# One decoder layer on one core: projections, gates and latents written ahead of the delta rule

## The chip, the cores and the metric

The kernel runs on one core of a Trainium2 chip. A core has a matrix engine (TensorE, PE in the rows), a vector engine (VectorE, DVE), a scalar engine (ScalarE, ACT), a general engine (GpSimd, POOL) and a queue engine (SyncE, SP) that here only issues DMAs. Each engine works through its own list of instructions in order and waits on semaphores for the others. The metric is device microseconds of one launch; lower is better.

## What is computed

One layer for 512 tokens of width 1024 in fp32. Cut to what the change touches:

```
proj = rmsnorm(x) @ w_in            # dq dk dv (4 heads of 128), dz, db, da, cq, ckv, kix, wix
q, k, v = silu(causal_conv4(dq, dk, dv));  q, k = l2norm(q) * 128**-0.5, l2norm(k)
# gated delta rule: a triangular solve (I + strict(beta k k^T decay)), then a scan with a state
o_dn = rmsnorm(delta_rule(q, k, v, beta, g)) * silu(dz)
# sparse attention: 8 heads, each query attends to the 128 keys that an indexer scores highest
score = sum_h wix_h * relu(q_idx_h . k_idx), causal;  idx = top_k(score, 128)
o_dsa = softmax(q_abs . c_kv[idx] / 8 + bias) @ c_kv[idx] @ w_uv
x = x + concat(o_dn, o_dsa) @ w_out
# then cross-attention into 256 memory tokens, a SwiGLU block, a last rmsnorm
```

## The kernel before

Most matmuls are in fp32r with every operand split into a high and a low part, three matmuls for one product (`mm3`, L149 to L151; for the gates L506 to L508). A weight block is loaded raw, ACT copies its high part (L141), and POOL or DVE subtracts to get the low part (`wl`, L142). Up to the output projection POOL does this for q, k and v of heads 2 and 3, all v, and the gates' weights.

The stages up to the output projection, by function:

- The indexer: L407/L408 multiply, L414 and L418/L419 (ACT and DVE) apply relu and weight, POOL adds into `masks` (L416), and L421 sets the future to a large negative number. `masks` holds the scores of three tiles of queries, 256, 384 and 512 keys wide.
- `project(kind, h)`: one head's k, q or v: 24 matmuls into one PSUM bank, L367 scales the bank out on DVE, then the four-tap convolution on ACT, DVE (L375, L378, L379) and POOL (L374, L380), and SiLU (L381). q, k of heads 0 and 1 come earlier than the change.
- `topk()`: a generator of 16 steps and a last one. A step takes the eight largest of each of three tiles (MAX8, L489) and strikes them out (L490, a load of the values and a MATCH_REPLACE8). The last step turns `masks` into an additive mask (L493). All of it is on DVE.
- `latents()`: q, k and v of the attention from the low-rank parts (`qd`, `kT`, `vt`; L533, L538 are plain fp32).
- `gates()`: SiLU of dz for four token tiles: 96 matmuls into four PSUM banks at once (L506 to L508), ACT (L512), POOL (L514).
- `prepare(h)`: norms of k and q, K K^T and K Q^T (L662), their products with the decay (L665), and a write of the result to DRAM (`n_d`).
- `diagonal_blocks()`: reads the 16x16 blocks of all heads back, inverts them with a serial chain of small DVE instructions (L691 to L710), writes them out (`x_d`, `y_d`, L712) and gathers them into the diagonals of `X` (SP's queue) and `Y` (ACT's queue, L717).
- `level(0)`, `level(1)`: the inverse grows from 16 to 32 to 64: L726 on PE, L728 on DVE, L734 on PE, L735 on DVE for four heads; level 0 ends with transposes of `Y` (L637) copied to `X` on ACT (L737). `last_level()`: 64 to 128, L745 to L758.
- `values_of(h)`: v with the tokens on the partitions (transposes L637, ACT L676).
- `recurrence()` and `attention()`, generators that run interleaved: four chunks of the scan (L781 to L825; the first chunk begins with L781 on `vtok`, `Y`), and logits (L582/L583), masks and maxima (L592), exponentials (L594), transposes (L598), sums (L607).

In the program text before, `prepare` of heads 0 and 1 comes first, then k and q of heads 2 and 3, each pair with its `prepare`, then the diagonal blocks and the levels, then latents, v, `values_of`, the gates, and the selection (`topk`) at the end. The text isn't the order on the engines: the program is built with a scheduler that simulates the engines and gives every instruction its place in its engine's list by when it is ready in that simulation. So the selection's DVE steps, last in the text, stand between the others from the moment when the scores are there.

What else couples the stages: the PSUM tiles are three `g` (the delta rule), two `lg` and two `tp` (projections, gates, latents; later the attention), one `o`. Weight blocks have three raw buffers and two for each split part. The attention's own buffers reuse those.

Of the kernel before, what the change touches and what calls it, by code (L numbers as in the profile page):

```python
# [81 lines left out]
def hybrid_block(ctx, tc, I, out):  # L82
# [85 lines left out]
    def weights(src, k0, kt, c0, cols, sub=None):  # L168
        return weights_split(*weights_raw(src, k0, kt, c0, cols), sub)
# [18 lines left out]
    xn = pool_of("xn")  # L188
# [113 lines left out]
    for w_, name in ((wq, "w_qidx"), (wu, "w_uq")):  # L302
        raw, _ = weights_raw(I[name][0], 0, 2, 0, 512)
# [46 lines left out]
    cvp = pool_of("cvp")  # L350

    def project(kind, h, bank="mm", sub=pool):
        def c(shape=(128, T)):
            n_t[0] += 1
            return cvp.tile(list(shape), FT, name=f"cp{n_t[0]}", tag="cp", bufs=6)

        m = {"q": h, "k": 4 + h, "v": 8 + h}[kind]
        wh, wl = weights(w_in, 0, 8, m * 128, 128, sub)
        o = dense(wh, wl, XH, XL, o=ps(bank))
        if kind == "k" and QK[h] is None:  # L360
            QK[h] = gdn.tile([128, 2, T], FT, name=f"QK{h}", tag=f"QK{h}")
        if kind == "v":
            vtok[h] = gdn.tile([128, NT, 128], FT, name=f"vtok{h}", tag=f"vtok{h}")
        dst = vtok[h].rearrange("p c d -> p (c d)") if kind == "v" else QK[h][:, 0 if kind == "k" else 1, :]
        cp = c((128, T + 4))
        pool.memset(cp[:, 0:3], 0.0)  # L366
        dve.tensor_tensor(cp[:, 3:T + 3], o, Rrow, op=OP.mult)  # L367
        a, b = c(), c()
        act.activation(a, cp[:, 0:T], AF.Identity, scale=par("conv_w", m))
        if m in (9, 11):  # L370
            d_ = c()
            act.activation(b, cp[:, 1:T + 1], AF.Identity, scale=par("conv_w", 12 + m))
            act.activation(d_, cp[:, 2:T + 2], AF.Identity, scale=par("conv_w", 24 + m))
            pool.tensor_tensor(b, b, d_, op=OP.add)  # L374
            dve.scalar_tensor_tensor(a, cp[:, 3:T + 3], par("conv_w", 36 + m), a, op0=OP.mult, op1=OP.add)  # L375
        else:
            act.activation(b, cp[:, 1:T + 1], AF.Identity, scale=par("conv_w", 12 + m))
            dve.scalar_tensor_tensor(a, cp[:, 2:T + 2], par("conv_w", 24 + m), a, op0=OP.mult, op1=OP.add)  # L378
            dve.scalar_tensor_tensor(b, cp[:, 3:T + 3], par("conv_w", 36 + m), b, op0=OP.mult, op1=OP.add)  # L379
        pool.tensor_tensor(a, a, b, op=OP.add)  # L380
        act.activation(dst, a, AF.Silu)  # L381
# [6 lines left out]
    for pr_ in range(4):  # L388
        q = ps()
# [51 lines left out]
    q = ps()  # L441
# [13 lines left out]
    for h in range(4):  # L455
        q = ps()
# [15 lines left out]
    q = ps()  # L472
# [12 lines left out]
    def topk():  # L485
        m8 = dsa.tile([128, 64], FT, name="m8")[:, :8]
        for it in range(16):
            for t in (3, 2, 1):
                dve.max(m8, score[t])  # L489
                dve.match_replace(score[t], m8, score[t], MARK)  # L490
            yield
        for t in (1, 2, 3):
            dve.tensor_scalar(score[t], score[t], MARK, -NEG, op0=OP.not_equal, op1=OP.mult)  # L493
        yield
# [25 lines left out]
    def latents():  # L520

        u = [gdn.tile([128, 512], FT, name=n, tag=f"zg{i}") for i, n in enumerate(("w_ukT", "w_uvT"))]
        sp.dma_start(u[0], I["w_ukT"])
        sp.dma_start(u[1], I["w_uvT"])
        for pr_ in range(4):
            ms = slice(pr_ * 128, (pr_ + 1) * 128)
            q = ps("mm")
            for k in range(2):
                mm3(q, wu[:, 0, k, ms], wu[:, 1, k, ms], cqh[k], cql[k], k == 0, k == 1)
            qd.append(dsa.tile([128, T], FT, name=f"qd{pr_}", tag=f"od{pr_}"))  # L530
            act.activation(qd[pr_], q, AF.Copy, scale=-0.125)
            q = ps("mm")
            pe.matmul(q, u[0][:, ms], ckvT, start=True, stop=True)  # L533
            kT.append(dsa.tile([128, T], FT, name=f"kT{pr_}", tag=f"ol{pr_}"))
            act.activation(kT[pr_], q, AF.Copy)
        for t in range(NT):
            q = ps("mm")
            pe.matmul(q, ckvT[:, t * 128:(t + 1) * 128], u[1], start=True, stop=True)  # L538
            vt.append(dsa.tile([128, 512], FT, name=f"vt{t}"))
            act.activation(vt[t], q, AF.Copy)  # L540
# [105 lines left out]
    def prepare(h):  # L646
        hc = slice(4 * h, 4 * h + 4)
        rk, cc = small(4), small(4)
        irk[h] = small(4)
        squares(tokens(QK[h][:, 0, :]), rk)  # L650
        rsqrt(rk, rk, 1.0)
        pool.tensor_tensor(cc, rk, rk, op=OP.mult)
        pool.tensor_tensor(cc, cc, beta[:, hc], op=OP.mult)
        pool.tensor_tensor(kdc[:, hc], cc, kd[:, hc], op=OP.mult)
        dve.reciprocal(irk[h], rk)
        for c in range(NT):
            act.activation(Dm[:, h, c, :], Dm[:, h, c, :], AF.Identity, scale=cc[:, c:c + 1])
        for c2 in range(2):
            q = ps("g")
            for e in range(2):  # L660
                c = 2 * c2 + e
                pe.matmul(q[:, 256 * e:256 * e + 256], QK[h][:, 0, c * 128:(c + 1) * 128],  # L662
                          QK[h][:, :, c * 128:(c + 1) * 128], start=True, stop=True)
            for k, dst in enumerate((NTt, A)):
                dve.tensor_tensor(dst[:, h, 2 * c2:2 * c2 + 2, :],  # L665
                                  q.rearrange("p (e k i) -> p e k i", e=2, k=2)[:, :, k, :],
                                  Dm[:, h, 2 * c2:2 * c2 + 2, :], op=OP.mult)
        sp.dma_start(bass.AP(tensor=n_d.tensor, offset=n_d.offset + h * 66048,
                             ap=[[128, 128], [16512, 4], [1, 128]]), NTt[:, h])
        squares(tokens(QK[h][:, 1, :]), ssq_[:, hc])  # L670
        pool.tensor_tensor(QK[h][:, 1, :], QK[h][:, 1, :], row[:, h, :], op=OP.mult)
# [157 lines left out]
    def steps(g, n):  # L829
        for _ in range(n):  # L830
            next(g, None)

    gt = topk()
    NTt = gp.tile([128, 4, NT, 128], FT, name="NTt", tag="NT")
    A = gp.tile([128, 4, NT, 128], FT, name="A", tag="A")
    prepare(0)
    prepare(1)
    for h in (2, 3):
        project("k", h)
        project("q", h)  # L840
        prepare(h)
    X = gp.tile([128, 4, NT, 128], FT, name="X", tag="X")
    Y = gp.tile([128, 4, NT, 128], FT, name="Y", tag="Y")
# [3 lines left out]
    for lev in range(2):  # L847
        level(lev)
    last_level()
    latents()  # L850
    for h in range(4):
        project("v", h)
    for h in range(4):
        values_of(h)
    for g_ in (gates(), gt):
        for _ in g_:
            pass
    cvp.release()
    xn.release()
    OGh = gp.tile([128, 4, T], FR, name="OGh", tag="NT")  # L860
    OGl = gp.tile([128, 4, T], FR, name="OGl", tag="OGl")
    core = recurrence()
# [52 lines left out]
    for k in range(KD):  # L915
        q = ps()
# [117 lines left out]
    g_ = I["g_final"]  # L1034
# [30 lines left out]
    for hf in range(2):  # L1065
        for t in range(NT):
            q = ps()
# [67 lines left out]
```

## Time and profile before

| | |
|---|---|
| device time, median of 3 runs | 860.77 us (859.05 to 861.39) |
| profiled execution | 862.52 us, of which span 860.7 us |
| mean granted clock of PE | 0.981 |
| busy in the span: PE, DVE, ACT, POOL | 828.9, 490.9, 366.5, 209.3 us |

The span is the time from the first to the last instruction in the profile; all times of the rows below count from its start. Busy shares say little by themselves: PE is busy 96% of the span, but DVE, with 57%, is busy without a break in one stretch and half idle in the rest. From about 282 us on (output projection, cross-attention, SwiGLU) PE is busy nearly all the time.

### The profile page before, as it was taken

How to read it: one execution, taken by the hardware profiler on the slowest of the kernel's cores; microseconds unless marked ns; L12 is line 12 of the kernel's file. 1: busy time of each engine (PE TensorE's matmuls, PEld its weight loads, DVE VectorE, ACT ScalarE, POOL GpSimd, SP SyncE). 2: the span in 40 equal slices, each digit the busy share in tenths (PEclk: the TensorE clock that was granted, in tenths of full speed). 3: DMA queues.
4: the chain of work that ended last, by engine and by line, in shares of the span. 5: the costliest groups of instructions: out<-in, count | busy, mean ns of one | idle time of the engine just before them, and what ended most of it. 6: DMA issues, size and time to landing. Idle time of an engine off the chain costs nothing.

```text
span 860.7 us, 11019 instructions
## 1 busy us (share of the span) xinstructions
PE 828.9 (96%) x4122; PEld 685.4 (80%) x4122; DVE 490.9 (57%) x817; ACT 366.5 (43%) x721; POOL 209.3 (24%) x217
## 2 busy tenths in 40 slices
PE   8998989899988999999999999999999999999996
PEld 7876757688776889898887888888888888888885
DVE  7787899974666555364555545553345553345542
ACT  6573774334577444353434443331122332233332
POOL 5448758426231132000002321110011110001122
PEclk9998999998899999999999999999999999999998
DMA  8541322116443534353323523333333333323302
GB/s 286 138 110 50 111 73 48 59 12 153 111 105 89 205 98 126 96 144 100 99 73 99 171 80 91 99 98 98 97 98 99 98 98 98 98 81 91 98 25 97
DMA packets 134940, 88.30 MB, mean 103 GB/s; under 512 B 10304, under 2 KB 122344, under 8 KB 134888
## 3 DMA queue, kind: packets, MB, share of 16 engines
q1 hardware_dynamic: 131848, 85.87, 34.4%
q10 hardware_dynamic: 3040, 1.75, 0.6%
q8 instruction: 32, 0.52, 0.2%
q14 instruction: 20, 0.16, 0.1%
HBM read 76.84 MB, written 4.99 MB: 95 GB/s over the span
## 4 chain that ended last, share of the span: by engine, by line
PE 78%; DVE 10%; ACT 4%; DMA 3%; issue 2%; POOL 2%; SPq 1%; ACTq 0%; POOLq 0%; DVEq 0%
PE ps L149 21%; PE ps L150 21%; PE ps L151 21%; DVE masks L490 1%; DVE m L489 1%; PE ps L607 1%; POOL masks L416 1%; PE ps L1080 1%; PE ps L1079 1%; PE ps L1078 1%; PE ps L954 1%; PE ps L956 1%; PE ps L955 1%; DVE cp L379 1%; PE ps L726 1%
## 5 line engine op out<-in xcount | busy, mean ns | idle before, releaser
L141 ACT ACTIVATE wh<-wraw 128x1024 fp32r<-128x1024 f32 x120 | 127.1, 1061 | 311.5 <-PE ps L150 172.6
L149 PE MATMUL ps<-XH,wh 128*128 128x512 f32 x512 | 200.8, 392 | 0.8 <-ACT wh L141 0.5
L151 PE MATMUL ps<-XH,wl 128*128 128x512 f32 x512 | 200.9, 392 | 0.4 <-POOL cp L366 0.4
L150 PE MATMUL ps<-XL,wh 128*128 128x512 f32 x512 | 200.1, 391 | 0.0
L142 DVE TENSOR_TENSOR wl<-wraw,wh 128x1024 fp32r<-128x1024 f32 x108 | 154.6, 1433 | 66.8 <-ACT wh L141 66.5
L149 PEld LDWEIGHTS ps<-XH,wh 128*128 128x128 f32 x512 | 96.2, 188 | 21.2 <-ACT wh L141 0.9
L151 PEld LDWEIGHTS ps<-XH,wl 128*128 128x128 f32 x512 | 96.2, 188 | 20.3 <-POOL cp L366 0.8
L150 PEld LDWEIGHTS ps<-XL,wh 128*128 128x128 f32 x512 | 96.2, 188 | 19.5 <-issue 0.2
L1049 POOL TENSOR_TENSOR t2k<-t2k,t2k 128x512 f32<-128x512 f32 x22 | 29.4, 1335 | 291.0 <-DVE t2k L1048 283.9
L258 POOL TENSOR_TENSOR acc<-acc,t2k 128x512 f32<-128x512 f32 x21 | 35.8, 1705 | 173.4 <-ACT t2k L257 173.1
L1048 DVE TENSOR_TENSOR t2k<-ps,row 128x512 f32<-128x512 f32 x22 | 15.2, 691 | 67.9 <-PE ps L151 67.9
L151 PE MATMUL ps<-HH,wl 128*128 128x512 f32 x128 | 50.0, 393 | 0.0
L149 PE MATMUL ps<-HH,wh 128*128 128x512 f32 x128 | 49.9, 390 | 0.0
L150 PE MATMUL ps<-HL,wh 128*128 128x512 f32 x128 | 49.6, 390 | 0.0
L1060 DVE TENSOR_TENSOR XR<-ps,XR 128x512 f32<-128x512 f32 x16 | 11.1, 692 | 51.9 <-PE ps L151 51.9
L1046 DVE TENSOR_TENSOR t2k<-ps,row 128x512 f32<-128x512 f32 x22 | 15.2, 691 | 36.0 <-PE ps L151 36.0
L142 POOL TENSOR_TENSOR wl<-wraw,wh 128x1024 fp32r<-128x1024 f32 x12 | 29.4, 2453 | 13.8 <-ACT wh L141 13.8
L489 DVE MAX8 m<-masks 128x8 f32<-128x512 f32 (+2 forms) x48 | 26.7, 556 | 4.3 <-POOL masks L421 3.4
L890 DVE TENSOR_TENSOR XR<-ps,XR 128x512 f32<-128x512 f32 x16 | 10.9, 689 | 31.2 <-PE ps L151 31.2
L150 PEld LDWEIGHTS ps<-HL,wh 128*128 128x128 f32 x128 | 24.0, 188 | 5.0
L151 PEld LDWEIGHTS ps<-HH,wl 128*128 128x128 f32 x128 | 24.0, 188 | 5.0
L149 PEld LDWEIGHTS ps<-HH,wh 128*128 128x128 f32 x128 | 24.1, 188 | 4.9
(398 smaller groups left out, 1673.0 us busy)
## 6 DMA issues: line engine op xcount, KB each, us to landing
wraw<-in_w_gate SPq DMA_DIRECT2D x22, 512.0 KB, 3.6
wraw<-in_w_up SPq DMA_DIRECT2D x22, 512.0 KB, 3.7
wraw<-in_w_down SPq DMA_DIRECT2D x20, 512.0 KB, 3.7
wraw<-in_w_in SPq DMA_DIRECT2D x16, 512.0 KB, 3.7
wraw<-in_w_xkv SPq DMA_DIRECT2D x16, 512.0 KB, 3.7
wraw<-in_w_out SPq DMA_DIRECT2D x8, 512.0 KB, 3.7
wraw<-in_w_xq SPq DMA_DIRECT2D x8, 512.0 KB, 3.8
wraw<-in_w_xo SPq DMA_DIRECT2D x8, 512.0 KB, 3.9
```

What stands on the lines that cost most here:

```text
L141: act.activation(h, src, AF.Copy)
L142: (sub or dve).tensor_tensor(l, src, f32(h), op=OP.subtract)
L149: pe.matmul(o, lh, rh, start=start, stop=False)
L150: pe.matmul(o, lh, rl, start=False, stop=False)
L151: pe.matmul(o, ll, rh, start=False, stop=stop)
L258: pool.tensor_tensor(self.acc, self.acc, s_, op=OP.add)
L489: dve.max(m8, score[t])
L890: dve.tensor_tensor(XR[m], o, XR[m], op=OP.add)
L1046: dve.tensor_tensor(s1, og_, Rrow2, op=OP.mult)
L1048: dve.tensor_tensor(s2, ou_, Rrow2, op=OP.mult)
L1049: pool.tensor_tensor(s1, s1, s2, op=OP.mult)
L1060: dve.tensor_tensor(XR[m], o, XR[m], op=OP.add)
```

## The change

The calls up to the recurrence are put in another order. No operation is added or removed, and no tile changes its size.

```
-    NTt, A = ...                      +    gt = topk()
-    prepare(0); prepare(1)            +    latents()
-    for h in (2, 3):                  +    for i, (kind, h) in enumerate(k2, q2, k3, q3, v0 .. v3):
-        project k, q of h             +        steps(gt, 1 if i % 2 else 2)
-        prepare(h)                    +        project(kind, h)
                                       +    gates() to its end, then topk to its end
                                       +    cvp.release(); xn.release()
                                       +    NTt, A = ...
                                       +    prepare(0) .. prepare(3)
     X, Y, memsets                          X, Y, memsets
     diagonal_blocks(), levels              diagonal_blocks(), levels
-    latents(); project v0 .. v3
     values_of(0 .. 3)                      values_of(0 .. 3)
-    gates() to its end, topk to its end
-    cvp.release(); xn.release()
     recurrence and attention               recurrence and attention
```

The lines themselves:

```
     gt = topk()
+    latents()
+    for i, (kind, h) in enumerate([(k, h) for h in (2, 3) for k in "kq"] + [("v", h) for h in range(4)]):
+        steps(gt, 1 if i % 2 else 2)
+        project(kind, h)
+    for g_ in (gates(), gt):
+        for _ in g_:
+            pass
+    cvp.release()
+    xn.release()
     NTt = gp.tile([128, 4, NT, 128], FT, name="NTt", tag="NT")
     A = gp.tile([128, 4, NT, 128], FT, name="A", tag="A")
-    prepare(0)
-    prepare(1)
-    for h in (2, 3):
-        project("k", h)
-        project("q", h)
+    for h in range(4):
         prepare(h)
```

What the scheduler makes of it is seen in each engine's list. On PE, where level 0 begins, before (`ps_1808` to `ps_1811` are the gates' four banks, `ps_1320` to `ps_1366` belong to level 0):

```order
L637 MATMUL ps_1799<-cst,vtok_1758 128x128 x4
L506 MATMUL ps_1808<-wh_1874,XH_88 128x512
L506 MATMUL ps_1809<-wh_1874,XH_88 128x512
L506 MATMUL ps_1810<-wh_1874,XH_88 128x512
L506 MATMUL ps_1811<-wh_1874,XH_88 128x512
L726 MATMUL ps_1341<-X,NTt 128x128 x4
L734 MATMUL ps_1348<-Y,cv_1325 128x128 x4
L734 MATMUL ps_1354<-Y,cv_1332 128x128 x4
L507 MATMUL ps_1808<-wl_1875,XH_88 128x512
L508 MATMUL ps_1808<-wh_1874,XL_96 128x512
L506 MATMUL ps_1808<-wh_1874,XH_89 128x512
```

The same place after the change (`ps_1412` is the gates' last bank, `ps_1806` to `ps_1858` belong to level 0):

```order
L507 MATMUL ps_1412<-wl_1506,XH_91 128x512
L508 MATMUL ps_1412<-wh_1505,XL_99 128x512
L726 MATMUL ps_1806<-X,NTt 128x128 x4
L726 MATMUL ps_1813<-X,NTt 128x128 x4
L726 MATMUL ps_1820<-X,NTt 128x128 x4
L726 MATMUL ps_1827<-X,NTt 128x128 x4
L734 MATMUL ps_1834<-Y,cv_1811 128x128 x4
L734 MATMUL ps_1840<-Y,cv_1818 128x128 x4
L734 MATMUL ps_1846<-Y,cv_1825 128x128 x4
L734 MATMUL ps_1852<-Y,cv_1832 128x128 x4
L637 MATMUL ps_1858<-cst,Y 128x128 x4
```

Before, the gates' matmuls stand between and behind those of level 0; now all 96 stand ahead of it, and level 0 follows with nothing between its own steps. Level 1 comes directly behind it, with the attention's first logits between its matmuls, and 49 rows of PE lie between the first logits (L582) and the first chunk of the recurrence (L781), where there were 20 before.

On DVE, where the diagonal blocks end (L710), before:

```order
L710 COPY cv_1300<-cv_1276 128x256
L490 MATCH_REPLACE masks<-m_1944,masks 128x256
L489 MAX m_1944<-masks 128x8
L375 SCALAR_TENSOR_TENSOR cp_1762<-cp_1759,prT,cp_1762 128x512
L490 MATCH_REPLACE masks<-m_1944,masks 128x512
L489 MAX m_1944<-masks 128x8
```

and after, up to level 0's first instruction (L728):

```order
L710 COPY cv_1786<-cv_1762 128x256
L490 MATCH_REPLACE masks<-m_991,masks 128x512
L489 MAX m_991<-masks 128x8
L493 TENSOR_SCALAR masks<-masks 128x512
L490 MATCH_REPLACE masks<-m_991,masks 128x384
L489 MAX m_991<-masks 128x8
L493 TENSOR_SCALAR masks<-masks 128x384
L490 MATCH_REPLACE masks<-m_991,masks 128x256
L493 TENSOR_SCALAR masks<-masks 128x256
L728 TENSOR_TENSOR cv_1811<-ps_1806,cst 128x512
```

Before, 36 more rows follow L710 up to the selection's last (L493), with level 0's L728 and L735 among them. Now the selection ends eight rows behind L710, and the levels come after it.

On POOL, where the indexer's scores are added up, before (`wl_1143` is the low part of a later head's weights):

```order
L416 TENSOR_TENSOR masks<-masks,rlb 128x256
L416 TENSOR_TENSOR masks<-masks,rlb 128x384
L416 TENSOR_TENSOR masks<-masks,rlb 128x256
L416 TENSOR_TENSOR masks<-masks,rlb 128x512
L142 TENSOR_TENSOR wl_1143<-wraw_1140,wh_1142 128x1024
L416 TENSOR_TENSOR masks<-masks,rlb 128x256
L416 TENSOR_TENSOR masks<-masks,rlb 128x384
L416 TENSOR_TENSOR masks<-masks,rlb 128x512
L416 TENSOR_TENSOR masks<-masks,rlb 128x384
```

and after:

```order
L416 TENSOR_TENSOR masks<-masks,rlb 128x256
L416 TENSOR_TENSOR masks<-masks,rlb 128x512
L416 TENSOR_TENSOR masks<-masks,rlb 128x384
L416 TENSOR_TENSOR masks<-masks,rlb 128x256
L416 TENSOR_TENSOR masks<-masks,rlb 128x512
L416 TENSOR_TENSOR masks<-masks,rlb 128x384
L416 TENSOR_TENSOR masks<-masks,rlb 128x512
L416 TENSOR_TENSOR masks<-masks,rlb 128x256
L416 TENSOR_TENSOR masks<-masks,rlb 128x384
L421 AFFINE_SELECT masks<-masks 128x128 x2
```

The split of weights has left its place among the additions into `masks`; the next one comes behind the last L421. On PE, a projection's 24 matmuls that stood among the indexer's matmuls have given their place to six plain fp32 matmuls of the latents, and stand behind the indexer now. From the fifth block of the output projection on, PE's lists are the same.

## Rows read from the trace of the kernel before

**Rows 1.** Windows: busy time of each engine, PE clock, DMA, by stage.

```profile
90.00:175.50 85.50, 76.76 (x322) 58.16 (x320) 82.15 (x188) 48.08 (x139) 52.83 (x57) 0.96 0.28 76
175.50:217.50 42.00, 41.00 (x296) 36.72 (x297) 25.97 (x60) 16.82 (x38) 19.33 (x22) 0.88 0.33 80
```

**Rows 2.** Windows of 5 us, the same columns.

```profile
80.00:85.00 5.00, 4.51 (x24) 4.41 (x23) 2.92 (x9) 4.32 (x12) 3.78 (x5) 0.54 0.11 32
...
210.00:215.00 5.00, 5.00 (x36) 4.15 (x33) 2.56 (x8) 3.24 (x11) 0.72 (x1) 0.50 0.82 197
...
235.00:240.00 5.00, 3.67 (x29) 3.26 (x28) 4.11 (x12) 3.83 (x19) 1.41 (x2) 1.00 0.59 141
```

**Rows 3.** Timeline of PE: start, length, instruction, count, idle before and releaser.

```profile
78.89 0.79 PE L407 MATMUL ps<-kid,qst3l 128*128 128x512 f32 x1 [2.51 <-DVE rlb L414]
...
159.62 0.74 PE L506 MATMUL ps<-wh,XH 128*128 128x512 f32 x1 [3.09 <-DVE cp L367]
...
175.59 2.92 PE L726 MATMUL ps<-X,NTt 128*128 128x128 f32 x24 [1.32 <-DMA Y<-y_d]
...
196.87 2.84 PE L726 MATMUL ps<-X,NTt 128*128 128x128 f32 x24
...
204.22 0.41 PE L745 MATMUL ps<-cst,Y 64*64 64x64 f32 x4
...
217.51 1.06 PE L781 MATMUL ps<-vtok,Y 128*128 128x128 f32 x4
...
282.47 0.50 PE L149 MATMUL ps<-odh,wh 128*128 128x512 f32 x1
```

**Rows 4.** Timeline of PE, 89 to 104 us: prices of single kinds of instruction.

```profile
89.46 0.40 PE L150 MATMUL ps<-XL,wh 128*128 128x512 f32 x1
...
94.24 0.39 PE L150 MATMUL ps<-XL,wh 128*128 128x512 f32 x1
...
101.93 0.60 PE L637 MATMUL ps<-cst,QK 128*128 128x128 f32 x4
102.37 1.89 PE L662 MATMUL ps<-QK 128*128 128x256 f32 x8
```

**Rows 5.** Timeline of POOL, in the indexer's stage.

```profile
75.02 2.35 POOL L142 TENSOR_TENSOR wl<-wraw,wh 128x1024 fp32r<-128x1024 f32 x1
```

**Rows 6.** Timeline of DVE, first and last of the selection, and level 1.

```profile
89.51 0.69 DVE L489 MAX8 m<-masks 128x8 f32<-128x512 f32 x1 [3.42 <-POOL masks L421]
...
166.64 2.51 DVE L710 COPY cv<-cv 128x256 f32<-128x256 f32 x1
...
185.68 0.56 DVE L489 MAX8 m<-masks 128x8 f32<-128x384 f32 x1
...
188.72 0.29 DVE L493 TENSOR_SCALAR masks<-masks 128x256 f32<-128x256 f32 x1
...
197.96 0.69 DVE L728 TENSOR_TENSOR cv<-ps,cst 128x512 f32<-128x512 f32 x1 [8.35 <-PE ps L726]
```

**Rows 7.** Groups of DVE by form, 89.4 to 189.6 us: busy, mean ns, idle before.

```profile
L379 DVE SCALAR_TENSOR_TENSOR cp<-cp,prT,cp 128x512 f32<-128x512 f32 x6 | 6.6, 1093 | 0.0
L378 DVE SCALAR_TENSOR_TENSOR cp<-cp,prT,cp 128x512 f32<-128x512 f32 x6 | 5.7, 943 | 0.0
...
L698 DVE TENSOR_TENSOR cv<-cv,cv 128x12 f32<-128x12 f32 x2 | 3.3, 1668 | 0.0
...
L728 DVE TENSOR_TENSOR cv<-ps,cst 128x512 f32<-128x512 f32 x4 | 2.7, 680 | 0.0
L735 DVE TENSOR_TENSOR Y<-Y,ps 128x512 f32<-128x512 f32 x4 | 2.7, 680 | 0.0
...
L375 DVE SCALAR_TENSOR_TENSOR cp<-cp,prT,cp 128x512 f32<-128x512 f32 x2 | 1.5, 740 | 0.0
...
L698 DVE TENSOR_TENSOR cv<-cv,cv 128x16 f32<-128x16 f32 x1 | 0.2, 160 | 0.0
```

**Rows 8.** Timeline of ACT: issue of the gathers into Y.

```profile
170.89 3.90 ACTq L717 DMA_DIRECT2D Y<-y_d  x8
```

More of the change, by code (lines that the diff above doesn't have):

```diff
@@ L849, in hybrid_block @@
     last_level()
-    latents()
-    for h in range(4):
-        project("v", h)
     for h in range(4):
         values_of(h)
[L855 to L859, printed above, removed]
     OGh = gp.tile([128, 4, T], FR, name="OGh", tag="NT")
```

## Prediction

> **What bounds the kernel now.** I read the stage windows first. From 90 to 175.5 us DVE is busy 82.15 of 85.5 us and PE 76.76; from 175.5 to 217.5 us PE is busy 41 of 42 us and DVE 25.97 [rows 1]. So up to the first level DVE sets the pace, and in the levels PE does. DVE's timeline shows why: the selection begins at 89.51 us, after DVE had idled 3.42 us for POOL's additions into the scores, and runs, mixed with convolutions, `prepare` and the diagonal blocks, to its last L493 at 188.72 us [rows 6]. The diagonal blocks' last instruction (L710) ends at 169.15 us in this mix, the gathers into `Y` are issued from 170.89 us [rows 8], and level 0 starts at 175.59 us, released by that DMA [rows 3]: 6.44 us from L710's end to level 0. Then the roles turn: DVE idles 8.35 us before level 1 [rows 6], since on PE the gates' matmuls stand between levels 0 and 1.
>
> PE's timeline gives the waits that the text order leaves: 2.51 us at the end of the indexer, 3.09 us before the gates (their fourth bank waits for a v projection's L367), 1.32 us before level 0 [rows 3]. After a wait the granted clock shows its lower level: 0.54 in 80 to 85 us. But 3.67 busy us out of five in 235 to 240 us, in short gaps, left it at 1.00, and it was at 0.50 in 210 to 215 us, in the last level, with PE busy throughout [rows 2].
>
> From 282.47 us the output projection runs [rows 3], with its order unchanged. So the question is when PE gets there.
>
> **The change, part by part.**
>
> *Start of the selection.* On POOL a split of 2.35 us stood among the additions [rows 5], while PE and DVE waited on that chain (the 2.51 and 3.42 us above). It now stands behind the last L421. The wait of 3.42 us covers the 2.35, so the selection starts 2.4 us earlier, at 87.1 us. At the least nothing, if the convolution or the `Dm` work on POOL takes its place; at the most 3.4 us, the whole idle time.
>
> *DVE's chain up to level 0.* The instructions are the same, but eight of level 0's (L728, L735: 680 ns each [rows 7], about 0.6 us from start to start, so 4.8 us) leave the selection's stretch. It lasted from 89.51 to 189.0 us, 99.5 us; now 94.7, so it ends at 181.8 us. The cost is in the place of L710: before, 36 rows followed it to the selection's end, now eight. By the end of the stretch before (185.68 to 189.0 us with one L735 in it [rows 6], plus a MATCH_REPLACE ahead of it) those eight take about 3.4 us, L493s included. L710 ends near 178.3 us, 9 us later than before, and with the same 6.4 us of DMA level 0 starts at **184.7 us**, 9 us later.
>
> This hangs on the DVE instructions that are stretched while POOL works. The convolution's L379 takes 1093 ns in the mean and L378 943, the same form in L375 740; two tiny L698 took 1668 ns, a third 160 [rows 7]; L710 took 2.51 us. That is 6×0.35 + 6×0.20 + 2×1.51 = 6.3 us of stretch, and with L710 some 8. I keep it, since POOL's list has the same splits near the same DVE rows. If it goes away level 0 starts at 176.5 us; if it doubles, at 193. [...]
>
> *PE up to level 0.* Behind the indexer PE now has 288 matmuls of projections, gates and latents. Their pace is 21 steps from 89.46 to 94.24 us, 0.2276 us each [rows 4]: 65.5 us. With them stand 13 groups of four transposes (0.44 from start to start), `prepare`'s 32 records of L662 (1.89 us for 8, so 7.6) and two plain latent matmuls (half as many records of twice the width, an estimate of 1.9): **80.7 us**. From about 88 us that is 169, with a few waits for POOL's splits and for banks 170 to 177. PE is done before level 0 may start at 184.7: the 9 us on the DVE chain become 8 to 14 us of PE standing idle, where it had 1.32 us before. What covered that wait were the gates' matmuls, and they are used up.
>
> *Levels.* Level 1 took 7.35 us (196.87 to 204.22), the last level with its few attention matmuls 13.3 us (204.22 to 217.51) [rows 3]. Level 0 is level 1 plus four groups of transposes and a copy to `X`: 7.35 + 1.8 + 0.6, and 2 us more, since after such an idle time the first 4 us run at half clock as at 80 us [rows 2]: 11.8. The attention's five pairs of logits and four transposes in level 1 are 14 instructions, at a transpose's 0.11 us [rows 4] 1.5 us; some 14 more stand in the last level, another 1.5. Together 11.8 + 8.8 + 14.8 = 35.4 us (rounded), against 42 us before, which held some half of the gates as well. The recurrence starts at 184.7 + 35.4 = **220.1 us**, 2.6 us later than at 217.51.
>
> *Recurrence to the output projection.* This took 282.47 − 217.51 = 65.0 us. Ahead of it lie now five more pairs of logits (128 to 512 columns, an estimate of 1.5 us by the 0.11 of 128 and the 0.23 of 512) and 22 more transposes (2.4): 3.9 us. PE's list also ends with the recurrence's last transposes directly before the output projection, with less of the attention to cover the last chunk: 0 to 3 us, I take 1. So 62.1 us, and the output projection would start at 282.2 us.
>
> *What is moved ahead of all this.* PE has six plain matmuls of the latents in the indexer's stage (12 records of 512 columns, by L662's price for half the width 5.7 us) where it had a projection (24×0.2276 = 5.5 us); that stage is bound by DVE and POOL, so it costs nothing there. The latents' buffers `qd` and `kT` are therefore ready early, and the attention isn't held by them; nor was it before. The attention's first loads wait for the weight buffers, which are free when the gates end, some 8 us before level 0. If the first logits (in the list they stand in level 1) find everything there, 1 to 2 us of the waits in level 1 and the last level are filled; I take 1.5.
>
> Sum: level 0 starts 9.1 us later (175.6 to 184.7); the levels take 6.6 less (42 to 35.4); the stretch of the recurrence 2.9 less (65.0 to 62.1); filled waits 1.5 less: 9.1 − 6.6 − 2.9 − 1.5 = **−1.9 us**. The profiled execution, 862.52 us with a span of 860.7, is 1.75 us above the median of 860.77. The difference counts from the median: 858.9, say **859.0 us**.
>
> **The rivals.** A measurement of this kernel can tell about 0.3%, 2.6 us, from no change.
>
> *The stretch on DVE shrinks (851 us).* With level 0 behind the selection, the small serial instructions of the diagonal blocks may fall where POOL has little to do. Then L710 is 8 us earlier, PE's idle time nearly vanishes, and level 0 starts at 176.5 to 177, bounded by PE. For it: L375 at 740 ns and the third L698 at 160 show that the same rows often meet nothing. Against it: POOL has the gates' splits in the same stretch. 859 − 8 = 851.
>
> *The clock (868 us).* Levels 0 and 1 have no other matmuls between their steps now. Their PE work is 16.9 us at full clock (64 records of L726 and L734 a level at 2.84/24 = 0.118 [rows 3], and level 0's transposes, 1.8). If the lower level that comes with the long idle time holds until the last level, which runs at it anyway, they take 33.8 instead of 11.8 + 8.8 = 20.6 us: +13, less 3 to 4 us that overlap what I charged already: +9. For it: 210 to 215 us at 0.50 while busy throughout. Against it: 235 to 240 us at 1.00 with gaps. It decides if the clock is still at 0.5 some 9 us after level 0 starts.
>
> *The diagonal blocks come late (867 us).* DVE's list is fixed by a simulation. If a convolution there waits for PE or POOL, or stretches double, L710 slips; each us slips level 0, since nothing is left to fill PE. From 4.6 us on (level 0 after 189.3 us) the kernel is slower by more than 0.3%; 8 us give 867. For it: L710 has only eight rows behind it. Against it: DVE worked without a break in this stretch before too, and the chain of the diagonal blocks kept its place in it.
>
> *The change does nothing that lasts (861 us).* The scheduler had dealt the selection between everything already, the sum of DVE work is the same, and gain and idle time cancel.
>
> **How the numbers follow.** Forecast 0.42 (855.5 to 862.5: 0.19 of it faster, 0.22 same, 0.01 slower); stretch shrinks 0.18; clock 0.15; late blocks 0.15; nothing 0.10 (0.01, 0.07, 0.02). Faster 0.38, same 0.29, slower 0.33. The range runs from 849.5, 1.5 us under the first rival, to 869, one over the clock's; outside lie the stretch's doubling with the clock together, and PE waits that vanish altogether.
>
> **What would show it.** The first MAX8 at 87 us; L710 ending at 178 and level 0 starting at 184 to 186 us, released by the DMA of `Y`, after 8 us or more in which PE waits; level 0 in 12 us, with a clock near 0.5 for its first 4; the recurrence's first L781 near 219 us; the first matmul of the output projection near 280.5. It is wrong if level 0 starts before 180 or after 190 us, if the levels take over 40 us, or if the recurrence, whose order I took from before, shows waits of its own.

## The result, and the profile after

The changed kernel takes 856.01 us (median of 5, 854.77 to 857.76) against 859.97 us before (median of 5). The ratio is 0.9945, with a 95% interval of 0.9919 to 0.997. On another chip, later, it was 857.67 us (median of 12) and the ratio 0.9974 (0.9948 to 1.0). So the change gains some 0.3 to 0.6%, about 2 to 4 us; the second interval reaches 1.0. The profiled execution took 855.63 us, its span is 853.8 us; that of before had 860.7. The profiles differ by 6.9 us, the medians by 4.0, and this turned out to be the most telling number of the study.

The stage windows of the kernel after, cut at its own stages (level 0 starts at 183.28 us, the recurrence at 216.76, the output projection at 275.55; columns as in [rows 1]):

```profile
75.00:90.00 15.00, 15.00 (x84) 11.93 (x84) 10.36 (x23) 13.75 (x40) 13.16 (x15) 1.00 0.01 2
90.00:183.28 93.28, 82.43 (x363) 64.93 (x362) 87.84 (x203) 49.68 (x142) 60.87 (x60) 0.95 0.28 77
183.28:216.76 33.48, 32.90 (x275) 29.49 (x275) 23.02 (x46) 18.40 (x45) 15.92 (x24) 0.93 0.67 159
216.76:275.55 58.79, 52.10 (x388) 39.54 (x387) 34.05 (x113) 37.13 (x133) 11.67 (x17) 1.00 0.44 131
```

At the end of the indexer PE no longer waits: it is busy 15.00 of 15 us with its clock at 1.00. Three 5 us windows of the kernel after, two of them those of [rows 2]:

```profile
80.00:85.00 5.00, 5.00 (x34) 3.97 (x33) 2.31 (x4) 5.00 (x18) 4.37 (x6) 1.00 0.00 0
165.00:170.00 5.00, 3.88 (x11) 2.80 (x10) 5.00 (x7) 0.00 (x0) 4.04 (x2) 0.50 0.00 0
210.00:215.00 5.00, 4.73 (x51) 3.96 (x50) 3.10 (x6) 4.54 (x12) 0.31 (x1) 1.00 0.66 154
```

Where 80 to 85 us had 0.54 and 210 to 215 us, in the last level, 0.50, both are now at 1.00. A new stretch at half clock stands at 165 us, in the gates. PE's timeline after, which answers to [rows 3]:

```profile
166.74 0.80 PE L507 MATMUL ps<-wl,XH 128*128 128x512 f32 x1 [1.12 <-POOL wl L142]
...
183.28 0.98 PE L726 MATMUL ps<-X,NTt 128*128 128x128 f32 x3 [4.40 <-DMA X<-x_d]
...
204.53 0.41 PE L745 MATMUL ps<-cst,Y 64*64 64x64 f32 x4
...
216.76 0.71 PE L781 MATMUL ps<-vtok,Y 128*128 128x128 f32 x4
...
274.69 1.10 PE L825 MATMUL ps<-cst,cv 128*128 128x128 f32 x4 [2.88 <-DVE cv L821]
275.55 0.48 PE L149 MATMUL ps<-odh,wh 128*128 128x512 f32 x1
```

Level 0 starts 7.7 us later than before, after 4.40 us in which PE waits for the gathers, and the output projection starts 6.9 us earlier. DVE's timeline after, which answers to [rows 6]:

```profile
85.89 0.69 DVE L489 MAX8 m<-masks 128x8 f32<-128x512 f32 x1 [3.58 <-POOL masks L421]
...
165.22 3.94 DVE L706 TENSOR_TENSOR cv<-cv,cv 128x64 f32<-128x64 f32 x2
...
175.73 0.39 DVE L710 COPY cv<-cv 128x256 f32<-128x256 f32 x1
...
179.38 0.29 DVE L493 TENSOR_SCALAR masks<-masks 128x256 f32<-128x256 f32 x1
```

The selection starts 3.6 us earlier, L710 ends at 176.12 us, 3.55 us ahead of the selection's end. The stretch beside POOL's work now falls on two small L706 (3.94 us for both, while POOL's timeline has two weight splits, 4.71 us from 164.33). L710, which ran beside a split on POOL before (166.50 to 168.91 us), takes 0.39 us where it took 2.51, with nothing on POOL beside it.

### The profile page after: what moved, and what is told of

The parts are those of the page before. It is cut to its first block, busy times and chain, and to the rows that moved or that the text cites. A ratio compares the mean times of both kernels' runs of the same rounds, so it can differ in the third digit from the quotient of the medians.

```text
span 853.8 us, 11022 instructions
## 1 busy us (share of the span) xinstructions
PE 824.2 (97%) x4122; PEld 679.5 (80%) x4122; DVE 489.6 (57%) x817; ACT 366.3 (43%) x721; POOL 211.4 (25%) x217
## 4 chain that ended last, share of the span: by engine, by line
PE 79%; DVE 12%; POOL 2%; ACT 2%; issue 2%; DMA 2%; SPq 0%; POOLq 0%; DVEq 0%; ACTq 0%
PE ps L149 21%; PE ps L150 21%; PE ps L151 21%; DVE masks L490 3%; DVE m L489 2%; DVE cp L378 1%; PE ps L607 1%; PE ps L1078 1%; PE ps L1077 1%; PE ps L1076 1%; PE ps L291 1%; PE ps L952 1%; PE ps L954 1%; PE ps L953 1%; POOL masks L416 1%
## 5 line engine op out<-in xcount | busy, mean ns | idle before, releaser
L149 PE MATMUL ps<-HH,wh 128*128 128x512 f32 x128 | 49.9, 390 | 0.0
```

The lines of the kernel that those rows point to most:

```text
L149: pe.matmul(o, lh, rh, start=start, stop=False)
```

## The experiments

Each experiment has its own ratio to the kernel before on its chip. Four versions in a first group, four in a second, four in a third; each group ran on one chip.

**What the text order does and doesn't do.** With the line that deals out the selection's steps between the projections left out, the lists of all five engines are the same as those of the changed kernel, row for row but for the numbers of lines and tiles. In the same way the kernel before gets the same lists with the whole selection moved to the front of the text. The scheduler places the steps by readiness; where they stand in the text has no effect here.

**The latents alone (e1).** Against the kernel before:

```
     gt = topk()
+    latents()
     NTt = ...
...
     last_level()
-    latents()
```

> The kernel before with one edit: the latents stand first, the rest of the text is as before. Theory A: the gain comes from the latents, which fill PE in the indexer's stage in place of a projection that needed a weight split on POOL; then the first MAX8 starts near 86 us, PE's clock is 1.00 from 75 to 90 us, and the time is 856 us (855 to 858), as after the whole change. Theory B: the gain comes from the projections and gates standing ahead of the delta rule; then the time stays at 860 us (858.5 to 861.5).

Measured: 852.71 us (median of 11), ratio 0.9923 (0.9895 to 0.9951). The first MAX8 starts at 87.08 us and the clock is 1.00 from 75 to 90 us, as theory A says. But this is more than the whole change brings, so neither theory has the size: the other part of the change, projections and gates ahead of the delta rule, takes some 2 to 5 us away again. The stage windows of this version show where, beside those of after:

```profile
75.00:90.00 15.00, 14.91 (x82) 11.47 (x81) 9.03 (x20) 12.60 (x36) 12.14 (x13) 1.00 0.01 2
90.00:184.03 94.03, 82.69 (x367) 66.48 (x366) 89.93 (x207) 48.80 (x140) 61.80 (x65) 0.94 0.28 76
184.03:215.18 31.15, 30.89 (x273) 28.45 (x273) 21.03 (x44) 18.92 (x46) 16.18 (x19) 0.95 0.58 139
215.18:273.10 57.92, 53.52 (x395) 40.98 (x393) 34.70 (x114) 39.24 (x137) 11.88 (x17) 1.00 0.46 131
```

Level 0 starts at 184.03 us here too, but the levels take 31.15 us in place of 33.48, and from the recurrence to the output projection PE idles 4.4 us in place of 6.7.

**Everything but the latents (e2).** Against the changed kernel:

```
     gt = topk()
-    latents()
     for i, (kind, h) in ...
         project(kind, h)
+    latents()
     for g_ in (gates(), gt):
```

> The changed kernel with the latents behind the eight projections instead of ahead of them. Theory A: the first MAX8 is back at 89 to 90 us, PE waits at the end of the indexer, and the time is 860 us or more (859 to 864). Theory B: 856 us (855 to 858), the gain is kept.

Measured: 859.42 us (median of 13), ratio 0.9992 (0.9965 to 1.002). The time is theory A's: with the latents late nothing is gained. Its windows, and level 0 in PE's timeline:

```profile
75.00:80.00 5.00, 2.32 (x8) 1.38 (x8) 2.00 (x3) 0.38 (x1) 5.00 (x4) 0.72 0.32 86
80.00:85.00 5.00, 4.52 (x25) 4.41 (x26) 2.91 (x9) 4.46 (x12) 3.78 (x5) 0.59 0.08 22
175.00:195.00 20.00, 1.82 (x12) 1.37 (x11) 13.13 (x24) 3.38 (x8) 14.70 (x19) 0.62 0.52 110
225.00:235.00 10.00, 10.00 (x58) 7.38 (x56) 3.65 (x9) 2.69 (x8) 1.73 (x3) 0.50 0.02 6
...
194.30 2.05 PE L726 MATMUL ps<-X,NTt 128*128 128x128 f32 x8 [16.29 <-DMA X<-x_d]
```

The wait at the end of the indexer is back, PE stands nearly idle from 175 to 195 us, and the last level is at half clock. But it isn't shown that the wait at the indexer's end makes the time. PE is through with its work ahead of level 0 at 178.0 us, no later than in the changed kernel (178.9). What comes later is level 0, since L710 ends at 187.29 us in place of 176.12. The profiled execution is also the slowest of the 13 (865.41 us; the others took 858.4 to 859.9).

**The diagonal blocks earlier and later (e8, e9).** Both are edits of the changed kernel, without the line that deals out the steps. e8 ties the last four selection steps behind L710; e9 ties the blocks' chain behind the selection's last step.

```
e8:  gates(); steps(gt, 12)
     ...
     Yb = diagonal_blocks()
+    dve.tensor_copy(m8[:, 0:1], Yb[:, 0, 0:1])
+    for _ in gt: pass
e9:  pool.memset(Xb...)                             # in diagonal_blocks()
+    dve.tensor_copy(Xb[:, 0, 1:2], score[1][:, 0:1])
+    pool.memset(Xb[:, 0, 1:2], 0.0)
```

> The changed kernel, with the last four of the 16 selection steps tied behind the diagonal blocks' last instruction (L710) by one copy of 128 elements. Theory: level 0's start is set by L710's place among the selection's steps; then L710 ends near 165 us, level 0 starts when the gates end, near 178.5 us in place of 183.3, without a drop of the clock behind an idle time, and the time falls by 4 to 6 us, to 851 us. Rival: what follows level 0 waits for the end of the selection (the masks of the attention) or for the small steps between DVE and ACT; then the time stays at 856 us.

> The changed kernel, with the diagonal blocks' chain tied behind the selection's last step by one copy of 128 elements. Theory: L710 ends 4 to 8 us later than at 176.1 us, level 0 starts that much later, and the time rises by as much, to 860 to 864 us. Rival (level 0's start has slack): 856 us.

Measured: e8 851.32 us (median of 7), ratio 0.9905 (0.9871 to 0.9939), the time that the theory gave. The way there isn't the theory's:

```profile
179.28 2.84 PE L728 MATMUL ps<-X,NTt 128*128 128x128 f32 x24
185.81 0.58 PE L728 MATMUL ps<-X,NTt 128*128 128x128 f32 x1 [3.69 <-DVE cv L730]
```

Level 0 (here L728) starts at 179.28 us, directly behind the gates. But DVE still has selection steps then, PE waits 3.69 us inside level 0, and its clock is at 0.50 from 185 to 190 us. The recurrence starts at 218.49 us, 1.7 us later than in the changed kernel. What is shorter is the stretch behind it, 53.9 us from there to the output projection in place of 58.8.

e9 852.63 us (median of 10), ratio 0.9912 (0.9883 to 0.994): not slower than the changed kernel but 3 to 5 us faster, against the theory and against its rival. PE's timeline of e9:

```profile
189.08 1.20 PE L730 MATMUL ps<-X,NTt 128*128 128x128 f32 x4 [9.90 <-DMA X<-x_d]
...
223.75 0.83 PE L785 MATMUL ps<-vtok,Y 128*128 128x128 f32 x6
...
272.58 0.66 PE L829 MATMUL ps<-cst,cv 128*128 128x128 f32 x4
272.99 0.48 PE L149 MATMUL ps<-odh,wh 128*128 128x512 f32 x1
```

Level 0 does start 5.8 us later than at 183.28, after 9.90 us of waiting, and the recurrence 7.0 us later. But the output projection starts 2.6 us **earlier**. From the recurrence to the output projection it takes 49.2 us in place of 58.8: more of the attention lies ahead of the recurrence, and the wait of 2.88 us before the recurrence's last transposes is gone. So "each us of level 0's start is a us of the end" is false here.

**The split among the additions (e10).** Against the kernel before, with the changed kernel on the same chip:

```
-        project("k", h)
+        project("k", h, sub=dve if h == 3 else pool)
```

> The changed kernel itself, so that the others have it on the same chip: 856 us (854.5 to 858).

> The kernel before with one edit: the weight split of k of head 3, which stood on POOL among the additions into the scores, is done by DVE. Theory A1 (that one split on POOL delays the scores, PE waits for it and its clock falls; this is what the early latents cure): the first MAX8 comes near 87 us, PE's clock is 1.00 in 75 to 90 us, and the time falls to about 856 us. Rival A2 (the early latents help in another way, as work that is moved out of a later stretch): the scores come earlier, but the time stays at 860 us.

Measured: the changed kernel 857.67 us (median of 12); e10 852.53 us (median of 11, 850.66 to 858.0), ratio 0.9928 (0.9896 to 0.996). The time falls, by more than A1 gave, and A2's time is missed as well. Two windows of e10, then rows of its PE, DVE and POOL timelines, and the last L421 of the kernel before:

```profile
75.00:80.00 5.00, 3.21 (x12) 2.46 (x13) 4.81 (x9) 1.63 (x4) 5.00 (x5) 0.80 0.38 108
80.00:85.00 5.00, 5.00 (x26) 5.00 (x26) 3.95 (x6) 4.64 (x15) 4.37 (x6) 0.51 0.00 0
...
76.65 0.50 PE L407 MATMUL ps<-kid,qst3d 128*128 128x512 f32 x1 [2.02 <-DVE rlb L414]
...
73.87 2.06 DVE L142 TENSOR_TENSOR wl<-wraw,wh 128x1024 fp32r<-128x1024 f32 x1
...
88.01 0.14 DVE L477 COPY sm<-ps 8x1 f32<-8x1 f32 x1 [4.07 <-PE ps L473]
88.59 0.67 DVE L489 MAX8 m<-masks 128x8 f32<-128x512 f32 x1
...
87.05 0.30 POOL L421 TENSOR_SCALAR_AFFINE_SELECT masks<-masks 128x128 f32<-128x128 f32 x1
...
89.19 0.29 POOL L421 TENSOR_SCALAR_AFFINE_SELECT masks<-masks 128x128 f32<-128x128 f32 x1
```

The scores are ready 2.1 us earlier (87.35 us in place of 89.48), so the split on POOL did hold them up. The first MAX8 starts only 0.9 us earlier, at 88.59 us, because DVE's list has L477 ahead of it, which waits for PE until 88.01 us. PE still waits at 75 to 80 us, and its clock still falls to 0.51. This doesn't speak against A1: the split now stands on DVE, in the same chain, directly ahead of the L414 for which PE waits 2.02 us. So whether PE's wait comes from the split is left untested. What else e10 gains lies behind this, in lists that the edit has reshuffled. Which part of them it is stays open.

**Both ideas together, and the opposite (f1, f2).** Both on top of e1. f1 ties selection steps behind L710 as e8 does (four steps; in a third group six), f2 ties the blocks behind the selection as e9 does.

```
f1:  steps(gt, 12)                                  # or steps(gt, 10)
     Yb = diagonal_blocks()
+    dve.tensor_copy(m8[:, 0:1], Yb[:, 0, 0:1])
f2:  for _ in gt: pass
     diagonal_blocks()                              # with the copy and the memset of e9
```

> The kernel before with the latents first and the last four selection steps tied behind the diagonal blocks. Theory C (the end is set by PE's work plus what PE loses to waits and to the lower clock; level 0's start matters only through the idle time ahead of it): the 6 us of idle time ahead of level 0 in the version with the latents first go down to 1 to 2, and the time falls by 2 to 4 us from that version's 852.7, to 850 us. Rival (the order of selection and blocks is given back in the recurrence): 852.7 us, no change.

> The kernel before with the latents first and the diagonal blocks tied behind the selection's last step. Theory C: level 0 starts 5 us later, PE idles as much more ahead of it, but the attention is further along when the recurrence starts and the recurrence loses less; the time is 851 to 854 us, as without the tie. Rival (each us of level 0's start is a us of the end, as the prediction had it): 857 to 859 us.

> As the version with the latents first and four selection steps behind the diagonal blocks (849.0 us), with six steps behind them. Level 0's start is then set by the gates' end alone, near 176.5 us; the selection ends about 7 us later, and the attention's masks with it. 848 to 850 us if the masks are still early enough, 852 or more if the attention waits for them.

Measured: f1 with four steps 849.04 us (median of 6), ratio 0.9868 (0.983 to 0.9905), as theory C said, and the fastest of all; its interval and that of e1 (0.9895 to 0.9951) just overlap. With six steps 856.16 us (median of 8), ratio 0.9935 (0.9908 to 0.9962): the selection then ends at 210.16 us in place of 193.48, and less of the attention stands ahead of the recurrence (4 pairs of logits and 2 transposes in place of 12 and 22). From the recurrence to the output projection it takes 67.1 us in place of 49.9. f2 868.01 us (median of 8), ratio 1.0081 (1.0051 to 1.011), outside what both theories gave. Its windows in the last level:

```profile
215.00:220.00 5.00, 4.57 (x51) 3.85 (x49) 3.10 (x10) 0.87 (x2) 0.51 (x1) 1.00 0.79 184
220.00:225.00 5.00, 2.92 (x20) 2.39 (x19) 1.61 (x7) 4.23 (x13) 1.19 (x2) 0.77 0.63 157
225.00:230.00 5.00, 5.00 (x25) 3.24 (x24) 1.13 (x4) 3.35 (x11) 1.67 (x3) 0.50 0.29 68
230.00:235.00 5.00, 5.00 (x30) 3.78 (x31) 2.40 (x4) 0.39 (x2) 0.00 (x0) 0.50 0.40 101
```

Level 0 starts at 193.25 us, 9.2 us later than in e1, and the levels take 44.6 us in place of 31.15. A wait inside the last level (PE busy 2.92 of 5 us) is followed by over 10 us at half clock. The last level at half clock is what the kernel before showed as well, and this led to the last question.

**The clock of the last level (b1, b2, d1).** The executions of the kernel before on two chips run from 854.3 to 865.9 us, and they go with the mean granted clock of the execution: 854.3 us at 0.994, 865.9 at 0.976. A straight line through the 51 executions has 6.1 us for each 0.01, with a correlation of −0.95 and −0.94 on the two chips; 19 executions on a third chip have 5.5 us and −0.95. So the kernel before was run again for its profile, and once with the waits of its last level filled:

```
     def last_level():
+        def fill(q):
+            pe.matmul(q[:, :256], ident, cst[:, 0:2, :].rearrange("p k c -> p (k c)"), start=True, stop=True)
...
             q = ps("g")
+            fill(q)
```

> The kernel before itself, for a second profile. Theory D (the spread of the kernel before, 854 to 866 us with a mean granted clock from 0.994 down to 0.976, is the clock in the levels): if this execution is near 855 us, its clock is 1.00 in the last level (205 to 222 us), where the first profile had 0.50; if it is near 860 or above, the clock is at 0.5 there again. Rival: the spread is somewhere else, such as in the indexer's stage at 75 to 85 us or behind 282 us.

> As the run above it, for a third profile of the kernel before: by theory D its time goes with the clock of the last level.

> The kernel before with 12 more matmuls (a constant of 128x256 in fp32, 0.43 us each, 5.2 us together) into the banks of the last level, ahead of its own matmuls, which overwrite them. Theory D: with the waits of the last level filled the clock stays at 1.00 in most executions, the mean clock rises from 0.984 to 0.988 or more, and the time is 856 to 860 us although PE does 5 us more. Rival (the clock has nothing to do with what fills the waits): the clock stays where it was and the time rises to 862 to 866 us.

Measured: b1 855.32 us at a clock of 0.994, b2 855.79 us at 0.990: the very kernel before, unchanged, as fast as the changed one. The two windows of b1 in the last level:

```profile
205.00:210.00 5.00, 4.47 (x56) 3.63 (x54) 2.52 (x10) 4.07 (x10) 1.64 (x4) 1.00 0.79 197
210.00:215.00 5.00, 5.00 (x50) 4.66 (x50) 3.89 (x10) 3.73 (x15) 1.64 (x2) 1.00 0.64 149
```

and the same two of the first profile of the kernel before, with PE's wait in its last level:

```profile
205.00:210.00 5.00, 4.46 (x49) 4.08 (x50) 1.93 (x5) 3.32 (x8) 2.47 (x4) 0.75 0.62 149
210.00:215.00 5.00, 5.00 (x36) 4.15 (x33) 2.56 (x8) 3.24 (x11) 0.72 (x1) 0.50 0.82 197
...
205.48 1.01 PE L745 MATMUL ps<-cst,Y 64*64 64x64 f32 x12 [0.85 <-DVE Y L735]
```

PE's timeline of b1 at the places of [rows 3]:

```profile
174.59 1.58 PE L726 MATMUL ps<-X,NTt 128*128 128x128 f32 x12 [1.33 <-DMA Y<-y_d]
...
204.51 1.01 PE L745 MATMUL ps<-cst,Y 64*64 64x64 f32 x12 [0.85 <-DVE Y L735]
...
212.94 0.28 PE L781 MATMUL ps<-vtok,Y 128*128 128x128 f32 x1
...
275.24 0.50 PE L149 MATMUL ps<-odh,wh 128*128 128x512 f32 x1
```

The same lists, the same wait of 0.85 us at the same matmul; in one execution the clock fell 2 us behind it and was at 0.50 from 207.5 to 221.2 us, past the end of the last level; in the other it stayed at 1.00. The last level takes 9.7 us (203.24 to 212.94) in place of 13.3, and the output projection starts at 275.24 us in place of 282.47. The lower clock cost 12.5 us of PE's time in the first profile and 2.8 in b1: 5.0 us less in the levels, 3.0 less ahead of them, 1.8 less behind. In b2 the stretch ahead of the levels lost 2.8 us to it and the time is only 0.5 us longer, so that part is nearly free. Theory D holds for the profiles. d1 holds half of it: its 12 executions have clocks of 0.986 to 0.992 where 13 of the 19 of before on the same chip have 0.982 or less, and its profile has 1.00 from 205 to 220 us; but the time is 863.09 us (median of 12), ratio 1.0007 (0.9982 to 1.0031). The expectation of 856 to 860 was missed; d1 takes 7.8 us more than b1. In d1's trace the 12 fills take 0.52 to 0.63 us each from start to start, 6.9 us together and not the 5.2 expected, about as much as the clock gives back.

**The profiles on one scale.** For each profile, PE's idle time and the time lost to the lower clock (busy time times one minus the clock) can be added up over windows of 2.5 us from 75 us to the first matmul of the output projection. An ordinary table, in us:

```
version                       idle   clock   output projection starts   start minus both
before, first profile         20.3   12.5    282.5                      249.7
before, b1                    22.0    2.8    275.2                      250.4
before, b2                    20.1    5.6    275.7                      250.0
changed kernel                18.1    4.9    275.6                      252.6
changed kernel, again         19.2    4.7    277.0                      253.1
e1 latents alone              16.1    4.4    273.1                      252.6
e2 all but the latents        26.0   12.2    285.4                      247.2
e8 four steps behind          14.7    8.3    272.4                      249.4
e9 blocks last                18.7    5.8    273.0                      248.5
e10 split of k3 on DVE        17.1   13.0    277.7                      247.7
f1 latents, four steps        14.2    5.8    268.2                      248.2
f1 latents, six steps         18.8    8.1    278.8                      251.8
f2 latents, blocks last       27.1   14.0    287.3                      246.2
d1 before, filled             18.7    8.9    285.0                      257.4
```

Without d1, whose last column holds 6.9 us of fills, the start varies by 19 us and the last column by 6.9. That column is PE's own work at full clock, so this is bookkeeping: it says how much PE lost, not why. It isn't exact, since the ends of matmuls in a profile are modelled. It sets the slow profiles apart (first of before, e2, f2), but among near ones it doesn't give the order: e1 loses 2.5 us less than e8 and starts the output projection 0.7 us later. Each row is one execution, and those of e2 and e10 are among the slowest of theirs.

Two more comparisons narrow it down. The first is the attention's work ahead of the recurrence. It is 5 pairs of logits and 2 transposes in the kernel before (65.0 us from the recurrence to the output projection, 62.3 in b1), 10 and 20 in the changed kernel (58.8), 12 and 23 in e8 (53.9), 12 and 22 in f1 with four steps (49.9), 14 and 22 in e9 (49.2). No run changes this alone, so it is a likely reason and not a shown one. The second is time at equal clock. Against the line through the executions of before on the same chip, taken at the version's own mean clock, the changed kernel in the second group is 0.3 us slower. e1 is 4.2 us faster, e8 7.0, e9 5.4, e10 4.8, f1 with four steps 8.3. So most of what these versions gain is not the clock's.

## Why the prediction was right or wrong

The time lies in the range, 3 us under the forecast of 859.0, and it moved the way that was forecast. Most terms came out near their forecast; that their sum has the right sign is luck, as shown below. The steps, one by one:

*The start of the selection*: forecast 87.1 us, measured 85.89. Right in kind: the split on POOL did hold the scores up, by 2.1 us in e10 where 2.4 were forecast. The forecast let PE's own wait at the indexer's end pay only through the selection's start. PE lost 3.4 us of idle time and 2.5 us of clock there before (75 to 90 us), and nothing after. Whether this loss has a price of its own is not settled. e1 is rid of it and faster at equal clock. But b1 and b2 have it too (3.3 and 2.8 us) and take 855 and 856 us, and in e2, where it is back, PE is through with its work ahead of level 0 as early as in the changed kernel.

*L710 and level 0*: forecast 178.3 and 184.7 us, measured 176.12 and 183.28. The chain from L710 to level 0 took 7.2 us in place of 6.4; the gathers into `X` were last, not those into `Y`. The step held to within 2.2 us. PE's 80.7 us up to there would have ended at 170 to 177; the gates ended at 178.9, as they waited for POOL's splits and ran at half clock around 165 us. PE's wait was thus 4.40 us in place of 8 to 14.

*The levels*: forecast 35.4 us, measured 33.48: 11.7 for level 0 (forecast 11.8), 9.6 for level 1 (8.8), 12.2 for the last (14.8). Level 0's first 4 us were at half clock, as forecast. *The recurrence*: forecast 62.1 less 1.5, measured 58.8, with a wait of 2.88 us before its last transposes where the forecast put 1.

*The sum*: −1.9 forecast, −6.9 from profile to profile, −4.0 from median to median. The term that was mis-sized is the price of the last level and of what follows. It was read as 13.3 us from a profile in which the clock was at 0.50 for 10 us of the last level, and carried over as if it were the work's own. Against b1, the kernel before with its clock at 1.00 in the levels, the terms are: level 0 +8.7 (forecast +9.1), levels 33.5 − 38.35 = −4.9 (−6.6), recurrence 58.8 − 62.3 = −3.5 (−2.9 − 1.5), in sum +0.3 (−1.9). Against this execution the schedule gains nothing: the forecast's gain of 1.9 us isn't there, and the measured gain came from the clock, which the forecast had only as a loss.

By this reckoning the gain of the median is the clock's. The 12 executions of the changed kernel in the second group have a mean clock of 0.9892 and a mean time of 857.8 us; the line through the executions of before gives 857.4 us at that clock. The changed kernel had 0.985 to 0.994 in all 17 executions; the kernel before falls to 0.976 to 0.982 in many. That the last level is what falls is shown in three profiles of before (0.50 in one, 1.00 in two), and e10's profile, with a mean clock of 0.980, has 0.50 there as well; for the other executions, of which only the mean clock is known, it is inferred. Why the changed order keeps it is not settled: 16 of the attention's transposes stand between the steps of its last level where there were two, which speaks for fewer waits there, and d1 shows that a fill keeps the clock; but the first profile and b1 show that the same wait can end either way.

*The rivals.* "The clock" had the right place but the wrong kernel: the half clock in the levels was more the price of before (5.0 us lost) than of after (2.3). In f2 and e2 the levels do lose 10.2 and 8.4 us to the clock, but in two falls with full clock between them (200 to 220 us), not in one that holds from level 0 on. "The stretch on DVE shrinks" came true by a part: L710 and L698 were not stretched, L706 was, by 3.5 us. "The diagonal blocks come late" did not come up, as L710 ended earlier than forecast. Its price, a us of the end for each us of L710, is what failed most clearly. In e9 L710 ends 5.9 us later and level 0 starts 5.8 us later, and yet the kernel gains, with more of the attention ahead of the recurrence. f2, with the same tie, loses. "The change does nothing that lasts" is what holds at equal clock.

## What to carry to other kernels

Before a stage is priced from one profile, look at the granted clock in it, and at the spread of the executions: when time goes with the mean clock, a second profile of the unchanged kernel costs little and says which part of the gain is the schedule's. In a stretch with two interleaved streams (here the recurrence and the attention) add up what the bounding engine loses from one end to the other; a later start of one stream may only swap the order of the work, as in e9. Such a sum says how much is lost and not why. And where a scheduler places instructions by readiness, compare the engines' lists before arguing from the text: dealing out the selection changed no row, while moving the latents alone took 0.8% off (e1).

## What the runs showed that was not expected

The granted clock of one program differs between executions with the same lists and the same waits: 2 us behind a wait of 0.85 us at the last level's first transposes it fell to 0.50 for 13.7 us in one execution and stayed at 1.00 in two others; the last level itself took 13.3 us and 9.7 us in the first two of them. The Trainium skill, page "TensorE: Matmul & The Clock Gate", section "Part 1: The HAM clock gate (the "warmup" mystery)", says of the start of a kernel that the number of matmuls at the lower rate varies from run to run. No run here shows that for the start; the traces show a variation of this kind in the middle of a kernel. The executions of the kernel before lie up to 11.5 us apart (854.3 to 865.9) and go with the mean clock.

Two tiny DVE instructions (128x64) took 3.94 us together while POOL split weights (4.71 us), and 0.42 us as a pair of the same kind 1.6 us earlier (L703). Which instructions are stretched changes with the list: L710 and L698 before, L706 after. The selection's MAX8 was not among them (0.69 us in the mean over the 128x512 ones of both kernels).
